# Two weight splits of a head pair placed behind the normalised q/k of its first and second tile, and the gate product made once for both heads on VectorE

## The chip, the cores and the metric

One core of a Trainium2 chip runs the whole program. The metric is device time in microseconds (us). All matrix products are made on TensorE (PE; PEld is its weight load), elementwise work on VectorE (DVE), ScalarE (ACT) and GpSimd (POOL); SyncE (SP) issues the loads from HBM. Each engine works through its own queue in order and waits there for the semaphores of the others.

## The reference

Two decoder layers over 512 tokens of width 1024. Each layer projects the normalised input to q, k, v and a gate for 16 heads of 64, runs two kinds of attention, multiplies by the gate, projects back and adds a gated embedding:

```
u = rms_norm(h, norm_g)
qa, ka, va, ga, fa, qb, kb, vb, gb = split(u @ w_in)
qa = rms_norm(heads(qa, 8), qk_g[0]);  ka = rms_norm(heads(ka, 8), qk_g[1])
oa = forgetting_attention(qa, ka, heads(va, 8), log_sigmoid(fa + b_f)) * silu(ga)
qb = partial_rope(rms_norm(heads(qb, 8), qk_g[2]));  kb likewise with qk_g[3]
ob = dilated_attention(qb, kb, heads(vb, 8)) * silu(gb)
h = h + concat([oa, ob]) @ w_out
h = h + (p_i @ w_ple) * sigmoid(rms_norm(h, ple_norm_g) @ w_ple_gate)
```

## The kernel before

**Precision.** Every float32 product is made of three matmuls. An operand is split into a high part (ScalarE, a rounding copy) and a low part (VectorE, the difference); `mm3` adds high x high, high x low and low x high. Activations live split in `X` and `Y` (high, low). Weights arrive in `raw` (3 buffers) and are split into `whi` (ScalarE, L157) and `wlo` (VectorE, L158), 5 buffers each. `W.pump()` makes the next split in a fixed list if its buffer is free; a split then also issues the load of a later `raw`.

**Head pairs.** A layer handles its 16 heads as 8 pairs `p`; pairs 0 to 3 are dilated (with rotary), 4 to 7 forgetting. The loop over `p` from 1 to 7 is a software pipeline: pair `p` is projected while the attention of pair `a = p - 1` is computed and that of pair `b = p - 2` is finished. A pair's weights are three pieces of w_q,k,v (1152, 1152 and 768 columns of `raw`) and one of the gate (1024). In the pass `p` the two "late" splits are those of the gate piece of `p` (1024) and of the first piece of pair `p + 1` (1152).

**The order on TensorE within a pass** is the order of the program (a wrapper keeps it): `pj(p, t)` projects the 128-token tile `t` onto 384 columns (24 matmuls). First `pj(p, 0)`, with `att_pv(b, 0)`, the product of probabilities and values of head 0 of pair `b`, inside it; then `pj(p, 1)` with `att_pv(b, 1)` inside; `pj(p, 2)`; `att_s(a)`, the scores of both heads of `a`; `pj(p, 3)`; `gate_mm`; and the transposes of the probabilities and of q and k (L91).

**The projections' results share two PSUM buffers**, `psA`. So `pj(p, 2)` may begin only when the first tile's result has been read, `pj(p, 3)` when the second's has, and the next pass's `pj(p + 1, 0)` when the gate's has (L482). A result is read by `ev(p, t)`: ScalarE squares it (L440, `sq`), VectorE reduces to mean squares (L442, L443, `ms`), GpSimd raises them to the power -1/2 (L445, `f`), and VectorE multiplies (L458, `z`). Beside this the value columns are scaled and split into `V2` (high L451 on ScalarE, low L452 on VectorE; two buffers by the parity of the pair, so that pair `p` overwrites what `att_pv(b, ...)` reads). Pairs below 4 then rotate `z` (L463 to L466; on GpSimd for tiles 0 to 2).

**Finishing pair b**: `att_pv` leaves a [128, 512] PSUM tile per head, whose two halves are added (L652 `ob` on ScalarE, L653 on VectorE) into 64 rows of `U[7]`; these rows are multiplied by the gate `U[5]` or `U[6]` (L655, a [64, 512] product per head, on GpSimd except for the last pair). `att_o` then splits `U[7]` into high (L658) and low (L659).

**Who sets the order on the other engines.** A scheduler orders each engine's instructions by program order and readiness. `with behind("A", "V")` ties instructions of the block behind the last instruction noted for ScalarE (`last["A"]`: L451 or a split of probabilities) and VectorE (`last["V"]`: L458, L482 or such a split). The closing step of the gate (L484, the function that `gate_evac` returns as `rest`) has no such tie.

Of the kernel before, what the change touches and what calls it, by code (L numbers as in the profile page):

```python
# [13 lines left out]
ALU = mybir.AluOpType  # L14
# [9 lines left out]
NPAIR = 8  # L24
# [177 lines left out]
def trunk(tc, ap):  # L202
    nc = tc.nc
    V, A, G, T = nc.vector, nc.scalar, nc.gpsimd, InOrder(tc, nc.tensor)
    ctx = ExitStack()
    with ctx:
# [11 lines left out]
        def ptile(pool, tag):  # L218
            return pool.tile([P, S], F32, tag=tag, name=tag)
# [19 lines left out]
        W = Weights(nc, wp, rp, specs)  # L239
# [4 lines left out]
        U = [cp.tile([P, S], F32, name=f"U{i}") for i in range(NK)]  # L244
# [128 lines left out]
        def behind(*engines):  # L373

            st = ExitStack()
            for e in engines:
                st.enter_context(tc.issue_after(last[e].ins))
            return st


        def square_acc(h, d, E=V):
            if d == 0:
                A.activation(acc, h, AF.Square)
            else:
                sq = tp.tile([P, S], F32, tag="sqh", name="sqh")
                done = A.activation(sq, h, AF.Square)
                E.tensor_tensor(acc, acc, sq, op=ALU.add)
                return done
# [7 lines left out]
        def finish_stats(pool, tag):  # L396
# [5 lines left out]
            r = sp.tile([P, NT], F32, tag="r", name="r")  # L402
            E = sp.tile([P, NT], F32, tag="E", name="E")
            rh = sp.tile([P, NT], F32, tag="rh", name="rh")
            V.tensor_scalar(m, ps[:, :NT], 1.0 / D, EPS, op0=ALU.mult, op1=ALU.add)  # L405
            G.tensor_tensor(r, m, mhalf.to_broadcast([P, NT]), op=ALU.pow)  # L406
            V.tensor_scalar(E, m, EPS, None, op0=ALU.mult)
            V.tensor_scalar(rh, r, 0.5, None, op0=ALU.mult)
            return r, E, rh

# [13 lines left out]
        def proj(l, p, t, u, ps, k0, k1):  # L424
            w = QW0 if p == 0 else QW
            for k in range(k0, k1):
                s, kk = min(k // 3, 2), k - 3 * min(k // 3, 2)
                wh, wl = W.get(("q", l, p, s))
                tk = slice(t * P, (t + 1) * P)
                mm3(ps[:, :w], u[0][:, k, tk], u[1][:, k, tk], wh[:, kk, :], wl[:, kk, :],  # L430
                    k == 0, k == NK - 1)
                if t == NT - 1 and k in (2, 5, 7):
                    W.done(("q", l, p, s))

        def evac_proj_a(l, p, t, ps, st):
# [6 lines left out]
            V.tensor_reduce(ms, sq, axis=AX.X, op=ALU.add)  # L442
            V.tensor_scalar(ms, ms, 1.0 / HD, st["E"][:, t:t + 1], op0=ALU.mult, op1=ALU.add)  # L443
            f = sp.tile([P, 4], F32, tag="f", name="f")
# [87 lines left out]
        def att_z(z):  # L532

            ps = pair(psM, "psM")
            for t in range(NT):
                for c in (0, 2):
                    o = (c // 2 * NT + t) * 64
                    flip([x[:, o:o + 64] for x in ps],
                         z[t][:, c:c + 2].rearrange("p h d -> p (h d)"))
            return ps  # L540
# [95 lines left out]
        def att_pv(a, j, pt=PT):  # L636
            ps = ptile(psS, "psS")
            v2 = V2[a % 2]
            for i in range(2):
                for kt in range(NT):  # L640
                    q0 = min(kt, 2)
                    if kt < 2:
                        rhs = pt[i][:, KOFF[kt]:KOFF[kt] + NT - kt]
                    elif kt == 2:
                        rhs = pt[i][:, 8:10 + 2 * j:1 + 2 * j]
                    else:
                        rhs = pt[i][:, 0:11 + 2 * j:10 + 2 * j]
                    T.matmul(ps[:, q0 * P:], v2[:, kt, j], rhs, start=(kt == 0 and i == 0),
                             stop=(kt == NT - 1 and i == 1))
            b = slice(64 * j, 64 * j + 64)  # L650
            tm = tp.tile([HD, S], F32, tag="ob", name="ob")
            A.activation(tm, ps[64:128], AF.Copy)  # L652
            V.tensor_tensor(U[7][b], ps[0:64], tm, op=ALU.add)  # L653
            E = V if a == NPAIR - 1 else G
            E.tensor_tensor(U[7][b], U[7][b], U[5 + a % 2][b], op=ALU.mult)  # L655

        def att_o(a, dst):
            A.activation(dst[0][:, a], U[7], AF.Copy)  # L658
            V.tensor_tensor(dst[1][:, a], U[7], dst[0][:, a].bitcast(F32), op=ALU.subtract)  # L659

# [24 lines left out]
        for l in range(DEPTH):  # L685
# [5 lines left out]
            def pj(p, t, k0=0, k1=NK):  # L691
                if k0 == 0:
                    cur[t] = ptile(psA, "psA")
                proj(l, p, t, u, cur[t], k0, k1)

            def ev(p, t):
                f = evac_proj_a(l, p, t, cur[t], st)
                zs[(p, t)] = evac_proj_b(l, p, t, cur[t], f)
# [45 lines left out]
            for p in range(1, NPAIR):  # L744
                a, b = p - 1, p - 2
                if p == 2:
                    log_forget(l)
                if p == 7 and l + 1 < DEPTH:
                    rope_tables(l + 1)
                if p == 1:  # L750
                    pj(p, 0)
                    pj(p, 1)
                    ev(p, 0)
                    att_qk(l, 0, att_z(zt(0)))
                    W.pump(2)
                else:
                    pj(p, 0, 0, 6)
                    att_pv(b, 0)
                    att_pt(1, tps)
                    with behind("A", "V"):  # L760
                        W.pump(2)
                    pj(p, 0, 6, NK)
                    pj(p, 1, 0, 3)
                    att_pv(b, 1)
                    pj(p, 1, 3, NK)
                    ev(p, 0)
                    att_o(b, oo)
                ev(p, 1)
                pj(p, 2)
                ev(p, 2)  # L770
                att_s(a)
                if NDIL <= p < NPAIR and a >= NDIL:
                    bias_rows(p)
                pj(p, 3)
                ev(p, 3)
                if p == NDIL:
                    cumulate()
                    bias_rows(p)
                gps = ptile(psA, "psA")
                gate_mm(l, p, u, gps, 0, NK)  # L780
                with behind("A", "V"):
                    W.pump()
                tps = [pair(psS, "psS") for _ in range(2)]
                att_tp(tps)
                pqk = att_z(zt(p))
                tpb = ptile(psA, "psA")
                att_tp2(tpb)
                rest = gate_evac(p, gps)
                att_pt(0, tps)
                att_pt2(tpb)  # L790
                with behind("A", "V"):
                    W.pump()
                att_qk(l, p, pqk)
                rest()

            a, b = NPAIR - 1, NPAIR - 2
            part(0, 0, 5)
# [166 lines left out]
```

## Time and profile before

| | |
|---|---|
| median of 3 runs | 768.87 us (761.44, 768.87 and 1137.11) |
| profiled execution | 761.52 us |
| its span, first to last instruction | 759.5 us |
| mean granted TensorE clock | 0.978 of full speed |
| PE busy | 711.9 us (94%) |
| DVE / ACT / POOL busy | 510.1 / 383.6 / 212.4 us |

The 2 us between the profiled execution's time and its span lie outside all instructions. The granted clock is a share of 2.4 GHz. Busy time is summed over stages that are bound by different things, so what a wait costs is read where it occurs.

### The profile page before, as it was taken

What the parts mean: (1) busy time and instruction counts of PE and PEld (TensorE: products, weight loads), DVE (VectorE), ACT (ScalarE), POOL (GpSimd) and SP (SyncE); (2) the same over time, 40 slices, a digit from 0 to 9 for tenths busy, and PEclk for the clock granted to TensorE, in tenths of its full rate; (3) what the DMA queues carried; (4) which work ended last, traced back from release to release, by engine and by line L of the source; (5) the groups of instructions that cost most, each with busy time, mean ns of one, the idle gap of its engine ahead of it and who ended that gap; (6) DMA issues with size and microseconds to landing.
All of it is one profiled execution on the core that took longest, in us unless ns stands there. A gap on an engine that the chain in (4) does not pass through costs nothing.

```text
span 759.5 us, 12111 instructions
## 1 busy us (share of the span) xinstructions
PE 711.9 (94%) x4424; PEld 630.7 (83%) x4424; DVE 510.1 (67%) x1228; ACT 383.6 (51%) x809; POOL 212.4 (28%) x354
## 2 busy tenths in 40 slices
PE   9998989897989899999999989898898989999997
PEld 8987979787978787887899889787787888888886
DVE  7878668675757486938737778585748577777443
ACT  8565546363736456625525647354545456564311
POOL 7363433322332511000004443524142323300000
PEclk9999999999999999999999999999999999999999
DMA  8513121212212043616323122120303031355211
GB/s 289 162 29 112 32 80 33 80 45 69 64 50 86 27 125 102 203 43 196 113 82 111 32 80 63 50 85 28 103 10 111 9 104 30 125 155 164 84 41 42
DMA packets 23946, 65.52 MB, mean 86 GB/s; under 512 B 4816, under 2 KB 6096, under 8 KB 23888
## 3 DMA queue, kind: packets, MB, share of 16 engines
q1 hardware_dynamic: 22576, 64.68, 27.4%
q8 instruction: 35, 0.57, 0.3%
q10 hardware_dynamic: 1312, 0.08, 0.1%
q14 instruction: 23, 0.19, 0.1%
HBM read 60.49 MB, written 4.19 MB: 85 GB/s over the span
## 4 chain that ended last, share of the span: by engine, by line
PE 71%; DVE 10%; ACT 8%; issue 5%; POOL 5%; ACTq 1%; DMA 0%; SPq 0%; POOLq 0%; DVEq 0%
PE psA L88 49%; PE psS L88 15%; PE psM L88 4%; DVE wlo L158 4%; POOL f L445 3%; ACT PT L621 2%; POOL U L655 2%; ACT whi L157 2%; ACT U L599 2%; PE psS L91 2%; DVE U L653 1%; PE psM L91 1%; DVE z L458 1%; ACT ob L652 1%; PE psA L91 1%
## 5 line engine op out<-in xcount | busy, mean ns | idle before, releaser
L88 PE MATMUL psA<-whi,X 128*128 128x384 f32 (+1 forms) x480 | 137.6, 355 | 20.5 <-DVE z L458 20.5
L88 PE MATMUL psA<-whi,Y 128*128 128x384 f32 (+1 forms) x480 | 135.1, 351 | 19.5 <-DVE z L458 19.5
L158 DVE TENSOR_TENSOR wlo<-raw,whi 128x1024 fp32r<-128x1024 f32 (+3 forms) x105 | 135.0, 1296 | 12.7 <-ACT whi L157 12.0
L157 ACT ACTIVATE whi<-raw 128x1024 fp32r<-128x1024 f32 (+3 forms) x105 | 105.4, 1020 | 68.5 <-PE psA L88 51.6
L88 PEld LDWEIGHTS psA<-whi,X 128*128 128x128 f32 x480 | 92.8, 199 | 23.7 <-issue 22.2
L88 PEld LDWEIGHTS psA<-whi,Y 128*128 128x128 f32 x480 | 91.3, 196 | 22.3 <-issue 21.3
L88 PE MATMUL psA<-Y,whi 128*128 128x512 f32 (+1 forms) x320 | 96.6, 385 | 0.5 <-DVE sqh L860 0.5
L88 PE MATMUL psA<-X,whi 128*128 128x512 f32 x304 | 95.7, 396 | 0.0
L655 POOL TENSOR_TENSOR U<-U,U 64x512 f32<-64x512 f32 x28 | 38.9, 1388 | 197.9 <-DVE U L653 197.9
L445 POOL TENSOR_TENSOR f<-ms,mhalf 128x4 f32<-128x4 f32 x64 | 64.7, 1011 | 97.1 <-DVE ms L443 87.3
L599 ACT ACTIVATE U<-U,mx 128x512 f32<-128x512 f32 (+3 forms) x128 | 70.6, 554 | 31.9 <-DVE mx L597 31.9
L88 PE MATMUL psA<-wlo,X 128*128 128x384 f32 (+1 forms) x240 | 84.5, 352 | 0.5 <-DVE wlo L158 0.5
L88 PE MATMUL psA<-wlo,Y 128*128 128x384 f32 (+1 forms) x240 | 83.3, 347 | 0.1
L601 POOL TENSOR_SCALAR U<-U,sm 128x512 f32<-128x512 f32 (+3 forms) x128 | 65.7, 533 | 25.5 <-DVE sm L600 25.2
L458 DVE TENSOR_TENSOR z<-psA,f 128x256 f32<-128x256 f32 x60 | 25.4, 424 | 66.3 <-POOL f L445 66.3
L88 PEld LDWEIGHTS psA<-Y,whi 128*128 128x128 f32 x320 | 58.4, 188 | 13.2 <-DVE sqh L860 1.2
L88 PEld LDWEIGHTS psA<-X,whi 128*128 128x128 f32 x304 | 56.5, 188 | 13.1 <-DVE sqh L860 0.5
L440 ACT ACTIVATE sq<-psA 128x256 f32<-128x256 f32 x56 | 21.3, 381 | 82.6 <-PE psA L88 76.3
L88 PE MATMUL psA<-Y,wlo 128*128 128x512 f32 (+1 forms) x160 | 61.3, 383 | 0.0
L88 PE MATMUL psA<-X,wlo 128*128 128x512 f32 x152 | 59.9, 394 | 0.0
L442 DVE TENSOR_REDUCE ms<-sq 128x4 f32<-128x256 f32 x56 | 23.3, 416 | 47.4 <-ACT sq L440 46.4
L406 POOL TENSOR_TENSOR r<-m,mhalf 128x4 f32<-128x4 f32 x4 | 4.7, 1184 | 161.1 <-DVE m L405 161.1
(191 smaller groups left out, 1319.9 us busy)
## 6 DMA issues: line engine op xcount, KB each, us to landing
raw<-in_wq_dram SPq DMA_DIRECT2D x28, 576.0 KB, 3.8
raw<-in_wg_dram SPq DMA_DIRECT2D x16, 512.0 KB, 4.2
raw<-in_wo_dram SPq DMA_DIRECT2D x16, 512.0 KB, 3.5
raw<-in_wpg_dram SPq DMA_DIRECT2D x16, 512.0 KB, 3.4
raw<-in_wq_dram SPq DMA_DIRECT2D x14, 384.0 KB, 3.1
U<-in_xT_dram SPq DMA_DIRECT2D x16, 256.0 KB, 3.7
raw<-in_wple_dram SPq DMA_DIRECT2D x4, 512.0 KB, 3.8
hs<-U SPq DMA_DIRECT2D x8, 256.0 KB, 3.1
```

The costliest lines, as they stand in the source:

```text
L88: return self.tc.keep_in_program_order(self.eng.matmul(*a, **k))
L91: return self.tc.keep_in_program_order(self.eng.transpose(*a, **k))
L157: self.nc.scalar.activation(hi, r, AF.Copy)
L158: eng.tensor_tensor(lo, r, hi.bitcast(F32), op=ALU.subtract)
L440: A.activation(sq, ps[:, :2 * P].rearrange("p (h d) -> p h d", h=4), AF.Square)
L442: V.tensor_reduce(ms, sq, axis=AX.X, op=ALU.add)
L445: G.tensor_tensor(f, ms, mhalf.to_broadcast([P, 4]), op=ALU.pow)
L458: last["V"] = V.tensor_tensor(z, ps[:, :2 * P].rearrange("p (h d) -> p h d", h=4), f[:, :, None].to_broadcast([P, 4, HD]), op=ALU.mult)
L599: A.activation(seg, seg, AF.Exp, bias=mx, scale=-1.0, accum_out=sm)
L601: G.tensor_scalar(seg, seg, sm, 1.0, op0=ALU.mult, op1=ALU.mult)
L621: last["A"] = A.activation(hi, src, AF.Copy)
L655: E.tensor_tensor(U[7][b], U[7][b], U[5 + a % 2][b], op=ALU.mult)
```

## The change

- `att_pv` no longer multiplies by the gate. `att_o` does it once, for both heads, as one [128, 512] product on VectorE in front of its two halves of the split.
- The two splits that `W.pump(2)` made ahead of the rest of `pj(p, 0)` are set apart: one behind the first tile's `ev`, one behind the second's, each tied behind that tile's L451 on ScalarE and L458 on VectorE.
- The closing step of the gate is tied behind the last instruction noted for VectorE.

```
             U[7][b] = ps[0:64] + tm
-            E = V if a == NPAIR - 1 else G
-            E.tensor_tensor(U[7][b], U[7][b], U[5 + a % 2][b], op=ALU.mult)
         def att_o(a, dst):
+            V.tensor_tensor(U[7], U[7], U[5 + a % 2], op=ALU.mult)
...
                     pj(p, 0, 0, 6)
                     att_pv(b, 0)
                     att_pt(1, tps)
-                    with behind("A", "V"):
-                        W.pump(2)
                     pj(p, 0, 6, NK)
...
                     ev(p, 0)
+                    with behind("A", "V"):
+                        W.pump()
                     att_o(b, oo)
                 ev(p, 1)
+                if p > 1:
+                    with behind("A", "V"):
+                        W.pump()
                 pj(p, 2)
...
                 att_qk(l, p, pqk)
-                rest()
+                with behind("V"):
+                    rest()
```

The order on TensorE, and that of the loads on SyncE, is the same in both kernels. On the other engines it moves. The names are the program's with a number: `U_95` is `U[7]`, `U_93` and `U_94` are the gates `U[5]` and `U[6]`, `Y_86` and `Y_87` the high and low part of `Y`, `V_116` a `V2` buffer.

VectorE in the pass p = 3 of the first layer, from the first head's sum to the low part of the attention output; first the kernel before:

```order
L653 TENSOR_TENSOR U_95<-psS,ob 64x512
L158 TENSOR_TENSOR wlo<-raw,whi 128x1024
L158 TENSOR_TENSOR wlo<-raw,whi 128x1152
L442 TENSOR_REDUCE ms<-sq 128x4
L653 TENSOR_TENSOR U_95<-psS,ob 64x512
L443 TENSOR_SCALAR ms<-ms,E 128x4
L452 SCALAR_TENSOR_TENSOR V_116<-psA,r,V_116 128x2x64
L458 TENSOR_TENSOR z<-psA,f 128x256
L659 TENSOR_TENSOR Y_87<-U_95,Y_86 128x512
```

The first tile's chain (L442, L443, L458) stands behind both splits and, by L443, behind the second head's sum. In the changed kernel:

```order
L653 TENSOR_TENSOR U_95<-psS,ob 64x512
L442 TENSOR_REDUCE ms<-sq 128x4
L443 TENSOR_SCALAR ms<-ms,E 128x4
L452 SCALAR_TENSOR_TENSOR V_116<-psA,r,V_116 128x2x64
L458 TENSOR_TENSOR z<-psA,f 128x256
L158 TENSOR_TENSOR wlo<-raw,whi 128x1024
L653 TENSOR_TENSOR U_95<-psS,ob 64x512
L656 TENSOR_TENSOR U_95<-U_95,U_94 128x512
L442 TENSOR_REDUCE ms<-sq 128x4
L452 SCALAR_TENSOR_TENSOR V_116<-psA,r,V_116 128x2x64
L443 TENSOR_SCALAR ms<-ms,E 128x4
L458 TENSOR_TENSOR z<-psA,f 128x256
```

The first tile's chain now precedes the 1024 split, and the product L656 stands ahead of the second tile's chain; the 1152 split and the low part (L658) follow behind that second L458.

ScalarE at the same place, before:

```order
L652 ACTIVATE ob<-psS 64x512
L157 ACTIVATE whi<-raw 128x1024
L157 ACTIVATE whi<-raw 128x1152
L440 ACTIVATE sq<-psA 128x256
L451 ACTIVATE V_116<-psA,r 128x2x64
L652 ACTIVATE ob<-psS 64x512
```

and in the changed kernel:

```order
L652 ACTIVATE ob<-psS 64x512
L440 ACTIVATE sq<-psA 128x256
L451 ACTIVATE V_116<-psA,r 128x2x64
L157 ACTIVATE whi<-raw 128x1024
L652 ACTIVATE ob<-psS 64x512
L440 ACTIVATE sq<-psA 128x256
L451 ACTIVATE V_116<-psA,r 128x2x64
L157 ACTIVATE whi<-raw 128x1152
```

Square and value copy of the first tile have come ahead of both high parts.

VectorE at the seam between two passes, from the gate's result (L482) to the split of the last weight piece (768), before:

```order
L482 TENSOR_TENSOR U_93<-psA,Rh 128x512
L484 SCALAR_TENSOR_TENSOR U_93<-sqh,U_93 128x512
L622 TENSOR_TENSOR PT_123<-psS,PT_122 128x8x64 x2
L549 SCALAR_TENSOR_TENSOR QQ_118<-psM,gq,QQ_117 128x4x64 x2
L622 TENSOR_TENSOR PT_123<-psA,PT_122 128x512
L158 TENSOR_TENSOR wlo<-raw,whi 128x768
```

and in the changed kernel:

```order
L482 TENSOR_TENSOR U_93<-psA,Rh 128x512
L622 TENSOR_TENSOR PT_123<-psS,PT_122 128x8x64 x2
L549 SCALAR_TENSOR_TENSOR QQ_118<-psM,gq,QQ_117 128x4x64 x2
L622 TENSOR_TENSOR PT_123<-psA,PT_122 128x512
L484 SCALAR_TENSOR_TENSOR U_93<-sqh,U_93 128x512
L158 TENSOR_TENSOR wlo<-raw,whi 128x768
```

The gate's closing step has gone from ahead of the split of the probabilities (L622) to behind it.

## Rows read from the trace of the kernel before

**Rows 1.** The page's list of engines: busy us, share of the span, instructions.

```profile
PE 711.9 (94%) x4424; PEld 630.7 (83%) x4424; DVE 510.1 (67%) x1228; ACT 383.6 (51%) x809; POOL 212.4 (28%) x354
```

**Rows 2.** Who waited for whom: us in total, times, the longest one.

```profile
PE psA L88 <- DVE z L458: 40.0, 12, 4.5
```

**Rows 3.** TensorE in the twelve stretches from the end of such a wait to the first score matmul (the 24 matmuls of pj(p, 2)): stretch, its us, PE busy (instructions), granted clock, DMA share, GB/s. The first and the last of nine at a clock below 1, the three at 1.00, and the sum of all twelve; then, from the same view, the 24 matmuls of pj(3, 3) in the first layer, ahead of which nothing waits.

```profile
73.29:79.21 5.92, 5.92 (x24) 0.71 0.00 1
...
249.68:254.05 4.37, 4.37 (x25) 1.00 0.00 0
447.90:452.27 4.37, 4.37 (x24) 1.00 0.02 4
...
587.04:592.72 5.68, 5.68 (x25) 0.75 0.01 3
621.76:626.13 4.37, 4.37 (x24) 1.00 0.01 2
sum 65.49, PE 65.47; mean PE 5.46
...
115.82:120.13 4.31, 4.31 (x27) 1.00 0.00 0
```

**Rows 4.** Timeline of TensorE in the pass p = 3 of the first layer: start us, us, engine, line, operation, out<-in, shape, count, [idle before <-releaser]. 93.34 begins pj(3, 0); 98.75 is its last matmul and the next one's first; 104.25 is the last of pj(3, 1); 107.76 the first of pj(3, 2); 113.68 begins the scores; 115.82 pj(3, 3).

```profile
93.34 0.43 PE L88 MATMUL psA<-whi,X 128*128 128x384 f32 x1
...
98.75 0.52 PE L88 MATMUL psA<-whi,X 128*128 128x384 f32 x2
...
100.50 1.46 PE L88 MATMUL psS<-PT,V 128*128 128x512 f32 x8
...
104.25 0.34 PE L88 MATMUL psA<-whi,X 128*128 128x384 f32 x1
107.76 0.41 PE L88 MATMUL psA<-whi,X 128*128 128x384 f32 x1 [3.17 <-DVE z L458]
...
113.68 1.50 PE L88 MATMUL psS<-KK,QQ 64*128 64x512 f32 x12
...
115.82 0.44 PE L88 MATMUL psA<-whi,X 128*128 128x384 f32 x1
```

**Rows 5.** Timeline of ScalarE in the same pass.

```profile
98.42 0.59 ACT L652 ACTIVATE ob<-psS 64x512 f32<-64x512 f32 x1
98.92 2.11 ACT L157 ACTIVATE whi<-raw 128x1024 fp32r<-128x1024 f32 x2
101.05 0.38 ACT L440 ACTIVATE sq<-psA 128x256 f32<-128x256 f32 x1
101.59 0.37 ACT L451 ACTIVATE V<-psA,r 128x128 fp32r<-128x128 f32 x1 [0.16 <-PE psS L88]
```

**Rows 6.** Timeline of VectorE in the same pass; the first two rows are of its beginning, the last of the third tile.

```profile
89.96 1.35 DVE L158 TENSOR_TENSOR wlo<-raw,whi 128x1152 fp32r<-128x1152 f32 x1
91.39 0.69 DVE L482 TENSOR_TENSOR U<-psA,Rh 128x512 f32<-128x512 f32 x1
92.78 0.69 DVE L484 SCALAR_TENSOR_TENSOR U<-sqh,U 128x512 f32<-128x512 f32 x1 [0.70 <-ACT sqh L483]
...
99.22 0.67 DVE L653 TENSOR_TENSOR U<-psS,ob 64x512 f32<-64x512 f32 x1
100.01 3.61 DVE L158 TENSOR_TENSOR wlo<-raw,whi 128x1024 fp32r<-128x1024 f32 x2
103.54 0.40 DVE L442 TENSOR_REDUCE ms<-sq 128x4 f32<-128x256 f32 x1
103.98 0.69 DVE L653 TENSOR_TENSOR U<-psS,ob 64x512 f32<-64x512 f32 x1
104.70 0.23 DVE L443 TENSOR_SCALAR ms<-ms,E 128x4 f32<-128x4 f32 x1
104.83 0.34 DVE L452 SCALAR_TENSOR_TENSOR V<-psA,r,V 128x128 fp32r<-128x128 f32 x1
107.19 0.42 DVE L458 TENSOR_TENSOR z<-psA,f 128x256 f32<-128x256 f32 x1 [2.01 <-POOL f L445]
107.53 0.68 DVE L659 TENSOR_TENSOR Y<-U,Y 128x512 fp32r<-128x512 f32 x1
...
114.20 0.42 DVE L442 TENSOR_REDUCE ms<-sq 128x4 f32<-128x256 f32 x1 [3.45 <-ACT sq L440]
```

**Rows 7.** Timeline of GpSimd in the same pass.

```profile
99.98 1.29 POOL L655 TENSOR_TENSOR U<-U,U 64x512 f32<-64x512 f32 x1 [11.24 <-DVE U L653]
104.81 1.26 POOL L655 TENSOR_TENSOR U<-U,U 64x512 f32<-64x512 f32 x1 [3.54 <-DVE U L653]
106.15 1.01 POOL L445 TENSOR_TENSOR f<-ms,mhalf 128x4 f32<-128x4 f32 x1
```

**Rows 8.** Groups of instructions by line and shape (busy us, mean ns | idle before): a VectorE step of the new product's shape, both inputs in SBUF.

```profile
L387 DVE TENSOR_TENSOR acc<-acc,sqh 128x512 f32<-128x512 f32 x28 | 19.3, 689 | 0.0
```

**Rows 9.** Timeline at the seam from the pass p = 3 to p = 4: the gate's result on VectorE and the first matmul of pj(4, 0) on TensorE.

```profile
126.55 0.69 DVE L482 TENSOR_TENSOR U<-psA,Rh 128x512 f32<-128x512 f32 x1
...
127.88 0.42 PE L88 MATMUL psA<-whi,X 128*128 128x384 f32 x1
```

**Rows 10.** Timeline inside pj(5, 0): the low part of the weight piece of 768 columns on VectorE and the first matmul that reads it.

```profile
167.73 0.96 DVE L158 TENSOR_TENSOR wlo<-raw,whi 128x768 fp32r<-128x768 f32 x1
...
168.75 0.44 PE L88 MATMUL psA<-wlo,X 128*128 128x384 f32 x1 [0.32 <-DVE wlo L158]
```

More of the change, by code (lines that the diff above doesn't have):

```diff
@@ L653, in att_pv @@
             V.tensor_tensor(U[7][b], ps[0:64], tm, op=ALU.add)
-            E = V if a == NPAIR - 1 else G
-            E.tensor_tensor(U[7][b], U[7][b], U[5 + a % 2][b], op=ALU.mult)
         def att_o(a, dst):
+            V.tensor_tensor(U[7], U[7], U[5 + a % 2], op=ALU.mult)
             A.activation(dst[0][:, a], U[7], AF.Copy)
@@ L759, in trunk @@
                     att_pt(1, tps)
-                    with behind("A", "V"):
-                        W.pump(2)
                     pj(p, 0, 6, NK)
@@ L766, in trunk @@
                     ev(p, 0)
+                    with behind("A", "V"):
+                        W.pump()
                     att_o(b, oo)
                 ev(p, 1)
+                if p > 1:
+                    with behind("A", "V"):
+                        W.pump()
                 pj(p, 2)
@@ L793, in trunk @@
                 att_qk(l, p, pqk)
-                rest()
+                with behind("V"):
+                    rest()
             a, b = NPAIR - 1, NPAIR - 2
```

## The prediction, made before the changed kernel ran

> **What bounds the kernel now.** I read the list of engines first. TensorE is busy for 711.9 of 759.5 us, VectorE for 510.1 [rows 1], so the time is TensorE's work plus its idle time, and a change on the other engines counts only through the latter. The list of waits says where that idle time is: twelve waits for the product z, 40.0 us together, the longest 4.5 [rows 2]. Twelve is six passes (p = 2 to 7) in two layers, one wait in each. Then I read the stretch behind each wait, because TensorE's clock need not be the same there: in nine of the twelve the 24 matmuls of pj(p, 2) ran with a granted clock of 0.71 to 0.75, that is partly at the lower level, 1.2 GHz, and partly at 2.4, and took 5.92 us in the first and 5.68 in the last of them; in the other three the clock was 1.00 and they took 4.37 [rows 3]. All twelve took 65.49; at 4.37 each they would take 52.44. So 13.05 us of slow matmuls go with the 40.0 of waiting.
>
> Last I read one pass, p = 3 of the first layer, on all four engines, to see what makes z late. TensorE ends pj(3, 1) at 104.59 and could begin pj(3, 2) at 104.42, one matmul spacing after the start of its last; it begins at 107.76, after z [rows 4]. The result that z reads was complete at about 99.1, where pj(3, 0) ended [rows 4]. Its chain starts late on ScalarE: the square waits behind both weights' high parts (2.11 us) and starts at 101.05 [rows 5]. It starts later still on VectorE, where both low parts run from 100.01 for 3.61 us and the reduction begins at 103.54; then the second head's sum (0.69) stands between L442 and L443. And on GpSimd the power waits for the second head's gate product, from 104.81 for 1.26, and starts at 106.15 [rows 6, 7]. Each of the three steps of the change takes one of these obstacles away.
>
> **The first tile's chain in the new order**, p = 3, with the durations of these rows.
> - ScalarE: ob ends at 99.01 [rows 5], the square runs 99.1 to 99.5. The value copy L451 doesn't move forward: it overwrites the buffer that att_pv of pair 1 is reading, and in the trace it was released by that product at 101.59 [rows 5]. So L451 ends at 101.96 in both orders.
> - VectorE: the first head's sum ends at 99.89, L442 takes 0.40 and L443 0.23 [rows 6], which with the hops of some 0.1 gives 100.7. GpSimd's power takes 1.01 [rows 7]: 101.8. L452 (0.34), ahead of z in the queue, has to wait for L451 and ends at 102.3; z takes 0.42 [rows 6] and ends at about 102.8.
> - TensorE wants the buffer at 104.42. The margin is 1.6 us; the wait goes altogether.
>
> **What lands behind it.** ScalarE makes the 1024 high part after L451 (half of 2.11, so until 103.0) and ob of the second head until 103.6. VectorE makes the low part: two took 3.61 us beside a GpSimd product, one of 1152 alone 1.35 [rows 6], so a single one lies between 1.35 and 1.9. I take 1.35, since GpSimd's product is gone: 104.4. The second sum (0.69) gives 105.1. The new product isn't in the trace; the nearest row of its shape, both inputs in SBUF, takes 0.689 [rows 8], and from below a half-height sum that reads PSUM 0.67 [rows 6], so 0.69: 105.8. Then L442, L452, L443 and the power: 108.0, and z of the second tile at 108.4. TensorE needs it for pj(3, 3). Without the wait pj(3, 2) runs from 104.42 for 4.31 to 4.37 [rows 3], the scores take 2.14 (113.68 to 115.82 [rows 4]), so at 110.9. The margin is 2.5.
>
> **The product.** GpSimd's two of 1.26 and 1.29 go [rows 7], VectorE gets one of 0.69. It costs nothing while it lies inside that margin of 2.5; uncovered, it would cost 12 x 0.69 = 8.3. For the last pair of each layer two half products on VectorE become one, with nothing to hide them: one less of about 0.69 for each layer on VectorE, but the first could already run ahead of the second sum, so I count nothing there.
>
> The trace shows the two engines in each other's way: two low parts took 3.61 with a product beside them, and at the pace of one alone would take 2.7 [rows 6, 7]. The Trainium skill, page Perfetto Trace Analysis, section Optimizing Scalar/DVE Operations, warns that GpSimd and VectorE share an SBUF read port, so that moving work between them might not help; on the contention these rows agree with it. By that rule the 1.26 that the power waited for would stay in the chain, 12 x 1.26 = 15.1 us less gain, and the sum would come to about 724. I don't take it, because the order puts the product behind the first tile's z.
>
> **The second split and the seam.** Behind the second z (108.4) VectorE has the 1152 low part (1.35) and the attention's low part (0.68): 110.4. The third tile's square is ready at about 109.3, so its L442 is up to 1.1 late; in the trace VectorE had been idle for 3.45 us ahead of this instruction [rows 6], and that idle time is the cover. The rows also overlap by up to 0.1 each, which would leave 0.3. A delay here passes on through softmax and the fourth tile to L482, which must free the buffer for the next pass. There the margin is 1.26 (L482 ends at 92.08, TensorE begins at 93.34 [rows 4, 6]), and 0.64 at the seam to p = 4, where it ends at 127.24 and TensorE begins at 127.88 [rows 9]. So a stall of between 0 and 0.5 us there; I take 0, and 12 x 0.5 = 6 as the upper end.
>
> **The gate's closing step** (0.69) leaves the head of the seam, along with the idle 0.70 in front of it [rows 6], so the splits of the probabilities may start 1.4 us earlier and absorb a late L482. It now stands ahead of the 768 low part, on which TensorE waited 0.32 in one pass [rows 10]; I allow 0.3 more in each layer, 0.6 together. Nobody needs its result until the product two passes on.
>
> **Loads.** The split of 1024 is followed by the load of the 768 piece of the next pair, which is split only after the next L482 (126.55 [rows 9]), some 20 us later; the one of 1152 by the load of the next gate, which is split a pass later. That both go out 2 to 9 us later costs nothing; a load that came too late would show as ScalarE waiting for it.
>
> **The sum**, against the profiled execution: 761.52 - 40.0 (waits) - 13.05 (slow matmuls) + 0.6 = 709.1. I say **709 us**. That execution equals the fastest of the three runs (761.44); the median (768.87) is 1% higher, and a median of the changed kernel may lie as much above my sum, at 716. The other ends: everything as bounded above without the seam and with VectorE's overlaps in my favour, 705; all seams at 0.5, 715.
>
> **Rivals.**
> - *The wait shrinks but stays.* z of the first tile hangs on L452, which hangs on ScalarE's L451, which hangs on TensorE's att_pv; if any of these falls behind by more than the 1.6 us of margin, TensorE still waits. For it speaks that L451 was released by TensorE in the trace [rows 5]; against it, that nothing but the square stands ahead of it now. At 1 us of waiting in each of twelve passes the sum is 721. I count no slow matmuls behind so short a wait: even of the twelve waits of the trace, 3.3 us in the mean, three were followed by a clock of 1.00 [rows 3].
> - *The clock stays low.* The nine slow stretches have another cause than the wait ahead of them, and only the 40.0 come back: 721.5. Against it: each of the nine follows a wait, and pj(3, 3), which nothing holds up, takes 4.31 us at a clock of 1.00 [rows 3].
> - *The splits move the wait to the seam: slower than before.* The two low parts and the product are 1.35 + 1.35 + 0.69 = 3.4 us of VectorE's time, 4.3 if the splits take 3.61 as beside GpSimd. If none of it fits into idle time, the third tile's chain, softmax and L482 are late by 4.3, TensorE waits 3.0 to 3.7 at each seam, the clock falls again (1.3 to 1.55 per pass), and that is 12 x 4.9 = 59 paid for 53 gained: 767. It decides from a delay of about 3.9 at the third tile's L442, where 3.45 us of idle time speak against it [rows 6].
>
> **Chances.** Forecast 0.78, the wait that stays 0.12, the clock 0.06, slower 0.04. The range from 704 to 723 takes in the first three down to the upper bounds and leaves out the last and a part of the second, some 0.12. A measurement of this kernel tells about 2% from no change. All cases but the last are 5% or more faster; the last lies within 2% or just beyond. So faster 0.95, same 0.04, slower 0.01.
>
> **What would show it.** In the trace of the changed kernel the waits of TensorE for z should be gone from the list, or far below 40; the mean granted clock should rise from 0.978 to nearly 1; a pass should take about 29.7 instead of 34.5 us (93.34 to 127.88 [rows 4, 9], less 3.17 and 1.55); L440 of the first tile should follow pj(p, 0) by under 0.1 us, and z should end 1 to 2 us before pj(p, 1) does. Of the seam: the time from L482's end to the next pass's first matmul, 1.26 before, should stay above zero, and the idle time ahead of the third tile's L442 should nearly vanish. The prediction is wrong if new waits for L482 or for a weight's low part appear in every pass, if the granted clock stays low in places without a wait, or if z of the first tile turns out to wait for something that these rows don't show, a PSUM or V2 buffer above all.

## The result, and the profile of the changed kernel

The changed kernel takes 712.23 us (711.52 to 713.09 in four runs), against 767.11 for the kernel before, the median of four runs, of which one took 1137.11. The ratio, which leaves that run out, is 0.931, with a 95% interval from 0.925 to 0.937: 6.9% less time. The prediction was 709, with a range from 704 to 723. The profiled execution took 712.22 us, its span is 710.4, and the granted clock is 0.999 in the mean, as foreseen.

The list of engines, as [rows 1]:

```profile
PE 699.4 (98%) x4424; PEld 618.4 (87%) x4424; DVE 501.8 (71%) x1240; ACT 382.3 (54%) x809; POOL 182.9 (26%) x326
```

TensorE does the same 4424 matmuls in 12.5 us less, and its idle time has gone from 47.6 us (759.5 less 711.9) to 11.0. Who waited for whom, TensorE's list from its top (us in total, times, longest), as [rows 2]:

```profile
PE psA L88 <- DVE wlo L158: 2.9, 8, 0.6
PE psM L88 <- DVE QQ L303: 1.5, 1, 1.5
PE psS L88 <- DVE PT L622: 0.6, 3, 0.2
```

The twelve waits for z, 40.0 us, are gone from the list. What heads it now is small: eight waits for a weight's low part, one ahead of the first pass and seven in the twelve passes. The matmuls that followed the waits, as [rows 3] (stretch of pj(p, 2), us, PE busy, clock, DMA share, GB/s; that of p = 3 in the first layer, the last, and the sum of the twelve):

```profile
99.81:104.11 4.30, 4.30 (x26) 1.00 0.34 91
...
572.24:576.55 4.31, 4.31 (x26) 1.00 0.39 122
sum 51.52, PE 51.52; mean PE 4.29
```

All twelve run at a clock of 1.00, at 2.4 GHz, and take 51.52 us instead of 65.49. They are even 0.9 below the 52.44 that the prediction took, for without a wait ahead of it each takes about 4.3, as pj(3, 3) did before [rows 3], and not 4.37.

The first tile's chain in the pass p = 3 of the first layer. ScalarE, as [rows 5], with the third tile's square as its last row:

```profile
94.52 0.38 ACT L440 ACTIVATE sq<-psA 128x256 f32<-128x256 f32 x1
96.97 0.37 ACT L451 ACTIVATE V<-psA,r 128x128 fp32r<-128x128 f32 x1 [2.07 <-PE psS L88]
97.24 1.05 ACT L157 ACTIVATE whi<-raw 128x1024 fp32r<-128x1024 f32 x1
...
104.22 0.39 ACT L440 ACTIVATE sq<-psA 128x256 f32<-128x256 f32 x1 [1.99 <-PE psA L88]
```

VectorE, as [rows 6], from the first tile's L443 to the third tile's reduction, and then the seam to p = 4 and the place in p = 6 that an experiment below is compared with:

```profile
96.22 0.23 DVE L443 TENSOR_SCALAR ms<-ms,E 128x4 f32<-128x4 f32 x1
97.37 0.35 DVE L452 SCALAR_TENSOR_TENSOR V<-psA,r,V 128x128 fp32r<-128x128 f32 x1 [0.92 <-ACT V L451]
97.64 0.41 DVE L458 TENSOR_TENSOR z<-psA,f 128x256 f32<-128x256 f32 x1
98.32 1.23 DVE L158 TENSOR_TENSOR wlo<-raw,whi 128x1024 fp32r<-128x1024 f32 x1 [0.26 <-ACT whi L157]
...
100.30 0.70 DVE L656 TENSOR_TENSOR U<-U,U 128x512 f32<-128x512 f32 x1
...
102.86 0.42 DVE L458 TENSOR_TENSOR z<-psA,f 128x256 f32<-128x256 f32 x1 [1.13 <-POOL f L445]
103.20 1.35 DVE L158 TENSOR_TENSOR wlo<-raw,whi 128x1152 fp32r<-128x1152 f32 x1
...
105.12 0.41 DVE L442 TENSOR_REDUCE ms<-sq 128x4 f32<-128x256 f32 x1
...
117.58 0.68 DVE L482 TENSOR_TENSOR U<-psA,Rh 128x512 f32<-128x512 f32 x1
...
183.73 0.68 DVE L622 TENSOR_TENSOR PT<-psA,PT 128x512 fp32r<-128x512 f32 x1
184.33 0.68 DVE L484 SCALAR_TENSOR_TENSOR U<-sqh,U 128x512 f32<-128x512 f32 x1
184.93 0.95 DVE L158 TENSOR_TENSOR wlo<-raw,whi 128x768 fp32r<-128x768 f32 x1
```

TensorE, as [rows 4] and [rows 9]: the first matmul of pj(3, 0), the first of pj(3, 3), the first of pj(4, 0), and in p = 6 the first that reads the 768 low part:

```profile
88.69 0.43 PE L88 MATMUL psA<-whi,X 128*128 128x384 f32 x1
...
106.24 0.44 PE L88 MATMUL psA<-whi,X 128*128 128x384 f32 x1
...
118.41 0.41 PE L88 MATMUL psA<-whi,X 128*128 128x384 f32 x1
...
185.94 0.44 PE L88 MATMUL psA<-wlo,X 128*128 128x384 f32 x1 [0.39 <-DVE wlo L158]
```

The first z ends at 98.05 and pj(3, 2) begins at 99.81, 1.76 later. L451 waited 2.07 us for TensorE's att_pv, with the square done long before, as foreseen. The second z ends at 103.28, and pj(3, 3) wants its buffer at 106.24. From pj(3, 0) to pj(4, 0) the pass takes 29.72 us, where it took 34.54. At the seam L482 ends at 118.26 and TensorE goes on at 118.41, 0.15 later; before, the margin there was 0.64 [rows 9]. Nothing is to spare at 0.15: as much lies between z and the matmul that waited for it in the kernel before (107.61 to 107.76 [rows 4, 6]).

Since TensorE's order is the same in both kernels, the spacing of each two matmuls in a row can be compared from start to start, which accounts for the 49.1 us by which the span fell: -41.9 for z, -12.4 for the matmuls that ran at the lower clock, +3.2 for the weights' low parts (all but 0.1 of it for the 768 piece), +1.1 and +0.4 for the splits of the probabilities (L622, L621), +0.8 for L482. The 0.3 that is left lies in spacings too small to name.

### The profile page after: what moved, and what is told of

The parts are those of the page before. It is cut to its first block, busy times and chain, and to the rows that moved or that the text cites. A ratio compares the mean times of both kernels' runs of the same rounds, so it can differ in the third digit from the quotient of the medians.

```text
span 710.4 us, 12211 instructions
## 1 busy us (share of the span) xinstructions
PE 699.4 (98%) x4424; PEld 618.4 (87%) x4424; DVE 501.8 (71%) x1240; ACT 382.3 (54%) x809; POOL 182.9 (26%) x326
## 4 chain that ended last, share of the span: by engine, by line
PE 64%; DVE 17%; ACT 8%; issue 4%; POOL 4%; ACTq 2%; DMA 0%; POOLq 0%; DVEq 0%
PE psA L88 42%; PE psS L88 16%; DVE wlo L158 5%; PE psM L88 4%; POOL f L445 3%; DVE PT L622 3%; ACT U L599 3%; ACTq L523 2%; ACT PT L621 1%; DVE U L597 1%; DVE U L653 1%; ACT whi L157 1%; ACT sqh L483 1%; DVE V L452 1%; DVE ms L442 1%
## 5 line engine op out<-in xcount | busy, mean ns | idle before, releaser
L158 DVE TENSOR_TENSOR wlo<-raw,whi 128x1024 fp32r<-128x1024 f32 (+3 forms) x105 | 122.8, 1171 | 13.3 <-ACT whi L157 13.2
L88 PE MATMUL psA<-whi,X 128*128 128x384 f32 (+1 forms) x480 | 130.5, 341 | 0.0
L88 PE MATMUL psA<-whi,Y 128*128 128x384 f32 (+1 forms) x480 | 129.3, 341 | 0.2 <-DVE U L482 0.2
L88 PEld LDWEIGHTS psA<-whi,X 128*128 128x128 f32 x480 | 87.9, 188 | 1.8 <-ACT whi L157 0.5
L88 PEld LDWEIGHTS psA<-whi,Y 128*128 128x128 f32 x480 | 87.5, 188 | 1.4 <-issue 0.4
L88 PE MATMUL psA<-wlo,X 128*128 128x384 f32 (+1 forms) x240 | 81.8, 341 | 1.7 <-DVE wlo L158 1.7
L88 PE MATMUL psA<-wlo,Y 128*128 128x384 f32 (+1 forms) x240 | 81.3, 339 | 1.2 <-DVE wlo L158 1.2
L458 DVE TENSOR_TENSOR z<-psA,f 128x256 f32<-128x256 f32 x60 | 25.4, 423 | 45.9 <-POOL f L445 45.9
L622 DVE TENSOR_TENSOR PT<-psS,PT 128x512 fp32r<-128x512 f32 (+1 forms) x58 | 37.1, 673 | 19.1 <-ACT PT L621 19.1
L88 PEld LDWEIGHTS psA<-wlo,X 128*128 128x128 f32 x240 | 45.2, 188 | 3.2 <-DVE wlo L158 3.2
L88 PEld LDWEIGHTS psA<-wlo,Y 128*128 128x128 f32 x240 | 45.1, 188 | 2.0 <-DVE wlo L158 2.0
```

The source lines that it names most:

```text
L88: return self.tc.keep_in_program_order(self.eng.matmul(*a, **k))
L158: eng.tensor_tensor(lo, r, hi.bitcast(F32), op=ALU.subtract)
L458: last["V"] = V.tensor_tensor(z, ps[:, :2 * P].rearrange("p (h d) -> p h d", h=4), f[:, :, None].to_broadcast([P, 4, HD]), op=ALU.mult)
L622: last["V"] = V.tensor_tensor(lo, src, hi.bitcast(F32), op=ALU.subtract)
```

## The experiments

Three questions. Which of the three parts of the change brings the gain? Which part gives some of it back in the new waits, and can it be had again? And are the margins what the prediction said? Times are medians; the kernel before took 766.2 to 767.4 beside them.

### The splits apart, without the other two parts

```
 (the changed kernel, with the product and the closing step as before)
             V.tensor_tensor(U[7][b], ps[0:64], tm, op=ALU.add)
+            E = V if a == NPAIR - 1 else G
+            E.tensor_tensor(U[7][b], U[7][b], U[5 + a % 2][b], op=ALU.mult)
         def att_o(a, dst):
-            V.tensor_tensor(U[7], U[7], U[5 + a % 2], op=ALU.mult)
...
-                with behind("V"):
-                    rest()
+                rest()
```

> The two splits are set apart as in the change, but the gate product stays per head on GpSimd and the gate's closing step is not tied. Theory (the splits alone held z of the first tile up; the product only added to it): z of the first tile ends before pj(p, 1) does, though GpSimd's first product may put the power off by 0.7 us; the twelve waits and the slow matmuls go, 712 us give or take 2. Rival (the product on GpSimd holds z up by itself, 1.26 us in each pass): TensorE still waits about 1 us in each of twelve passes, 722 to 727 us.

711.59 us (710.88 to 711.94), ratio 0.930 (0.924 to 0.935). So the splits alone bring all that the whole change brings; nothing of the waits for z remains. The margin of the first z is smaller, though, down to 0.27 and 0.30 us in the passes p = 5, and a reason is seen in this kernel's trace, p = 3. VectorE:

```profile
95.61 1.02 DVE L443 TENSOR_SCALAR ms<-ms,E 128x4 f32<-128x4 f32 x1
...
100.65 1.18 DVE L443 TENSOR_SCALAR ms<-ms,E 128x4 f32<-128x4 f32 x1
```

and GpSimd:

```profile
95.33 1.28 POOL L655 TENSOR_TENSOR U<-U,U 64x512 f32<-64x512 f32 x1 [10.67 <-DVE U L653]
...
100.51 1.29 POOL L655 TENSOR_TENSOR U<-U,U 64x512 f32<-64x512 f32 x1
```

L443, a step on four columns that takes 0.23 us in the changed kernel, starts just after GpSimd's product and ends when the product ends (96.63 and 96.61; 101.83 and 101.80). It stands still for the rest of it.

### The product alone

```
 (the kernel before)
             V.tensor_tensor(U[7][b], ps[0:64], tm, op=ALU.add)
-            E = V if a == NPAIR - 1 else G
-            E.tensor_tensor(U[7][b], U[7][b], U[5 + a % 2][b], op=ALU.mult)
         def att_o(a, dst):
+            V.tensor_tensor(U[7], U[7], U[5 + a % 2], op=ALU.mult)
```

> Only the product moves to VectorE, both splits stay ahead of the first tile's chain. Theory: the power of the first tile starts when L443 ends, 1.2 us earlier, so the twelve waits shrink from 40 to about 25 us in all but stay; and since the slow matmuls belong to the length of the wait ahead of them, waits of 2 us leave the clock at 1.00 and 13 us come back too: about 734 us. Rival (the clock falls whatever the wait's length): 747 us. Second rival (moving work between GpSimd and VectorE brings nothing): 761 us.

729.40 us (728.05 to 730.52), ratio 0.953 (0.946 to 0.960), 5 us better than the expectation had it, with 16.8 us of waiting where it had 25. TensorE's list of waits, its first line:

```profile
PE psA L88 <- DVE z L458: 16.8, 12, 2.8
```

VectorE in p = 3, both splits (the row has two instructions) and L443:

```profile
97.96 2.50 DVE L158 TENSOR_TENSOR wlo<-raw,whi 128x1024 fp32r<-128x1024 f32 x2
...
101.53 0.23 DVE L443 TENSOR_SCALAR ms<-ms,E 128x4 f32<-128x4 f32 x1
```

and GpSimd's power for the first tile of that pass:

```profile
101.84 1.01 POOL L445 TENSOR_TENSOR f<-ms,mhalf 128x4 f32<-128x4 f32 x1 [15.12 <-DVE ms L443]
```

The two splits take 2.50 instead of 3.61 [rows 6], and the power starts after L443 and no longer behind a product of 1.26 [rows 7]. So the two products on GpSimd held z up twice in this pass: 1.1 us on VectorE, where the first split stood still beside the first product, and about 1.2 in GpSimd's own queue. Ten of the twelve passes look like it; in those of p = 2 both delays are shorter. As an estimate, 12 x 2.3 = 28 us is therefore an upper end, against 23.2 less waiting (40.0 to 16.8). Matched matmul by matmul with the kernel before, 11.1 of the 32.9 us between the two spans are the clock. Two of the twelve stretches of pj(p, 2); the second is the only slow one:

```profile
72.78:77.14 4.36, 4.36 (x25) 1.00 0.01 6
168.82:174.74 5.92, 5.92 (x24) 0.71 0.05 20
```

Alone the splits gain 55 us and the product 37, both together 58 (the run without the tie, below): they remove the same wait. Once the splits are apart, the product's place is worth little.

### The tie of the closing step alone

```
 (the kernel before)
                 att_qk(l, p, pqk)
-                rest()
+                with behind("V"):
+                    rest()
```

> The kernel before with only the gate's closing step tied behind the split of the probabilities. Theory: the twelve waits for z are untouched, and what little TensorE waits for the 768 low part is absorbed by them: 761 us give or take 2. Rival (the 1.4 us that the head of the seam gains carry through to z): 745 us.

759.27 us (756.92 to 765.50), ratio 0.992 (0.989 to 0.996): 0.8% less time, well below 2% but beyond its interval. The time is the expected one, the reason is not quite: the waits for z, which were to be untouched, fall from 40.0 to 32.8 us. All the same, ten of the twelve stretches behind them now run partly at the lower clock, where it was nine. Two of them, with their granted clock:

```profile
178.36:182.72 4.36, 4.36 (x25) 1.00 0.01 4
210.99:216.88 5.89, 5.89 (x25) 0.72 0.00 1
```

and the waits ahead of these two, from TensorE's timeline:

```profile
178.36 0.41 PE L88 MATMUL psA<-whi,X 128*128 128x384 f32 x1 [3.05 <-DVE z L458]
...
210.99 0.66 PE L88 MATMUL psA<-whi,X 128*128 128x384 f32 x1 [2.26 <-DVE z L458]
```

The longer wait is followed by the full clock, the shorter one by the lower. So the length of a wait doesn't decide by itself whether the clock falls behind it.

### The change without the tie

```
 (the changed kernel)
                 att_qk(l, p, pqk)
-                with behind("V"):
-                    rest()
+                rest()
```

> The change without the tie of the gate's closing step. Theory A (the step in front of the 768 low part is what makes TensorE wait 2.9 us for that part): the waits for the 768 low part fall back to about 0.6 us and the time is 709 to 711 us. Theory B (L482 comes late at the seam now, 0.1 to 0.9 us ahead of TensorE instead of 0.6 to 1.3, and the closing step at the head of the seam would wait 0.7 for ScalarE and put off the splits of the probabilities and the 768 low part by up to 1.4): the waits grow, 715 us or more.

708.48 us (708.00 to 709.75), ratio 0.926 (0.921 to 0.930). Beside the changed kernel on one chip it is 708.92 against 712.75 (below). The tie, which takes 0.8% off the kernel before, costs the changed one 3.8 us. TensorE's list of waits, the line on the low parts:

```profile
PE psA L88 <- DVE wlo L158: 0.8, 3, 0.3
```

VectorE in p = 6, to be held against the same place in the changed kernel (183.73 to 184.93 above):

```profile
181.21 0.69 DVE L484 SCALAR_TENSOR_TENSOR U<-sqh,U 128x512 f32<-128x512 f32 x1 [0.70 <-ACT sqh L483]
...
183.80 0.68 DVE L622 TENSOR_TENSOR PT<-psA,PT 128x512 fp32r<-128x512 f32 x1
184.40 0.95 DVE L158 TENSOR_TENSOR wlo<-raw,whi 128x768 fp32r<-128x768 f32 x1
```

and TensorE:

```profile
185.41 0.44 PE L88 MATMUL psA<-wlo,X 128*128 128x384 f32 x1
```

Without the tie L484 is over before the probabilities' split; with it, it stands straight ahead of the 768 low part, which TensorE needs next, and moves it back by 0.5 us relative to the pass's begin. In five of the eight waits of the changed kernel (p = 4, 6 and 7 in the first layer, 6 and 7 in the second) L484 is the instruction ahead of the split. In the two of p = 5, 0.58 us each, it is a second L549, which has moved ahead of the split; the eighth, 0.20, lies before the first pass and is there in the kernel before too.

This run and the one with the splits alone differ only in the product, and neither has the tie: 708.48 against 711.59, on one chip. That is the product's worth once the splits are apart: 3.1 us.

### One split ahead of the first tile, or both behind the second

The 1024 split back in its old place:

```
                     att_pt(1, tps)
+                    with behind("A", "V"):
+                        W.pump()
                     pj(p, 0, 6, NK)
...
                     ev(p, 0)
-                    with behind("A", "V"):
-                        W.pump()
                     att_o(b, oo)
```

> The change, but the split of 1024 goes back to its old place ahead of the first tile's chain; only the one of 1152 stays behind z of the second tile. Theory (z of the first tile has 1.1 to 1.8 us of margin in the profile of the changed kernel, and ScalarE's value copy, which waits for TensorE, hides most of a split): z comes up to 1.4 us later, so TensorE waits 0 to 0.3 us per pass, and the time is 711 to 715 us. Rival (each split ahead of the chain costs its own length): 12 x 1.3 us more, about 728 us.

717.68 us (717.49 to 718.26), ratio 0.939 (0.933 to 0.946): 2.7 us above the expectation. The list shows no wait for z; its margin is 0.15 to 0.83 us, thinner by up to about the length of the split, and in the three passes where it is 0.15 the matched matmuls behind it lose 0.2 us each. Most of the loss is elsewhere, by TensorE's list of waits:

```profile
PE psA L88 <- DVE wlo L158: 3.3, 8, 0.6
PE psA L88 <- DVE U L482: 1.7, 3, 0.7
```

Both behind the second tile:

```
                     ev(p, 0)
-                    with behind("A", "V"):
-                        W.pump()
                     att_o(b, oo)
...
                     with behind("A", "V"):
-                        W.pump()
+                        W.pump(2)
```

> The change, but both splits stand behind z of the second tile. Theory (the seam is the next tight place: L482 ends only 0.1 to 0.9 us ahead of TensorE's next matmul in the changed kernel): the third tile's chain, softmax and L482 come about 1.3 us later, TensorE waits some 0.4 to 1.2 us at each of twelve seams, 720 to 725 us, with waits for L482 in the list. Rival (idle time of VectorE ahead of the third tile still covers it): 712 us as the change.

718.76 us (718.02 to 719.03), ratio 0.940 (0.935 to 0.946): 6.5 us lost against the changed kernel, 3.2 of it at the first matmul behind L482, as expected in kind and less in size (720 to 725). TensorE's list:

```profile
PE psA L88 <- DVE wlo L158: 3.9, 9, 0.6
PE psA L88 <- DVE U L482: 2.1, 3, 1.0
```

So there is a place for one split behind each tile and for no second one behind the second: two together there make the third tile's chain late (in p = 3 its L442 starts 17.5 us after the pass's begin instead of 16.4), and that is passed on to L482, as the prediction's seam step has it.

Why one split ahead of the first tile is nearly as dear, its trace shows in part. Matched with the changed kernel, 2.4 of its 5.4 us lie at the first matmul behind L482 and 0.6 at z; the rest is spread over smaller waits. VectorE and, at the seam behind it, TensorE in its pass p = 3:

```profile
101.37 0.69 DVE L658 TENSOR_TENSOR Y<-U,Y 128x512 fp32r<-128x512 f32 x1 [0.70 <-ACT Y L657]
...
119.04 0.41 PE L88 MATMUL psA<-whi,X 128*128 128x384 f32 x1 [0.44 <-DVE U L482]
```

The attention's low part (L658) has come to stand ahead of the second tile's chain, where VectorE idles 0.70 us for ScalarE's high part; in the changed kernel it stands behind the 1152 split and waits for nothing. From the pass's begin the second z ends 1.0 us later and L482 0.6 later than in the changed kernel. The same 0.70 stands in all twelve passes of both runs, so not all that either loses is the split's own length; no run here takes the two apart.

### The gate's tanh and closing step behind the 768 split

If VectorE's order ahead of the 768 split is what costs, ScalarE's should too: the tanh (L483) stands ahead of that split's high part and of the copies of the probabilities.

```
 (the changed kernel)
             last["V"] = V.tensor_tensor(gt, ps, Rh, op=ALU.mult)
-            A.activation(th, gt, AF.Tanh)
-            return lambda: V.scalar_tensor_tensor(gt, th, 1.0, gt, op0=ALU.add, op1=ALU.mult)
+
+            def close():
+                A.activation(th, gt, AF.Tanh)
+                V.scalar_tensor_tensor(gt, th, 1.0, gt, op0=ALU.add, op1=ALU.mult)
+            return close
...
-                with behind("V"):
+                with behind("A", "V"):
                     rest()
```

> The change, but the gate's tanh on ScalarE goes with its closing step behind the split of the 768 piece. Theory (the waits for the 768 low part come from what stands ahead of it at the head of the seam): the splits of the probabilities start 0.6 us earlier, the waits for the 768 low part go, and the time is 707 to 709 us, as without the tie or a little better. Rival (the tie itself isn't what costs): 712 us.

706.37 us (705.93 to 707.23), ratio 0.925 (0.921 to 0.929), 0.6 us below the 707 that was expected at best. Only one wait for a low part of a pass is left in its list:

```profile
PE psA L88 <- DVE wlo L158: 0.2, 1, 0.2
```

and in p = 6, VectorE's order is (L486 is the closing step here):

```profile
182.22 0.68 DVE L625 TENSOR_TENSOR PT<-psA,PT 128x512 fp32r<-128x512 f32 x1
182.82 0.94 DVE L158 TENSOR_TENSOR wlo<-raw,whi 128x768 fp32r<-128x768 f32 x1
...
184.47 0.68 DVE L486 SCALAR_TENSOR_TENSOR U<-sqh,U 128x512 f32<-128x512 f32 x1
```

The split comes 3.3 us after the pass's begin instead of 5.2 (its end less the first matmul of pj(6, 0), which is at 180.47 here and at 180.71 in the changed kernel).

### On top of that, the attention output's split later

The margin at L482 is still 0.15 to 0.9 us there (from the pass p = 2 on). Moving att_o from behind the first tile to the fourth (between its value copy and its z) takes its three steps out of the third tile's way.

```
 (the kernel with the late tanh)
                     ev(p, 0)
                     with behind("A", "V"):
                         W.pump()
-                    att_o(b, oo)
...
+                f3 = evac_proj_a(l, p, 3, cur[3], st)
+                if p > 1:
+                    with behind("W"):
+                        att_o(b, oo)
+                zs[(p, 3)] = evac_proj_b(l, p, 3, cur[3], f3)
```

> As the one with the late tanh, and the gate product with the split of the attention output moved on from behind the first tile to the fourth tile, where VectorE waits for GpSimd's power. Theory (what keeps L482 late is the work ahead of the third tile's chain): the third tile's chain and softmax start 0.5 us earlier, the seam's margins come back to 0.5 us or more, and the time falls by about 1 us more, to 706 to 708 us. Rival (the two steps then stand ahead of L482 and take the margin again): 709 us or more.

710.18 us (709.77 to 711.00), ratio 0.929 (0.925 to 0.934): 3.8 worse than without, and the rival was right. In the fourth tile these steps stand in VectorE's queue ahead of L482, whose margin falls to 0.05 to 0.59 us. Of the 2.8 us between the two profiles 1.4 lie at the first matmul behind L482 and most of the rest at splits of the probabilities. The idle time that the third tile gains is not the one that the seam needs.

### The same three on one chip

The changed kernel, the one without the tie and the one with the late tanh once more, side by side.

> The changed kernel itself once more, beside the next two on the same chip: 712 us.

> The change without the tie of the gate's closing step, once more: 708.5 us, 3 to 4 us below the change, if what was measured before isn't the difference between two chips; level with it otherwise.

> The change with the gate's tanh and closing step both behind the 768 split, once more: 706 to 707 us, 5 to 6 us below the change and 2 below the one without the tie; level with them if the differences are the chips'.

712.75 (711.88 to 713.77), 708.92 (708.09 to 710.10) and 706.38 (705.82 to 707.07); the ratios to the kernel before are 0.931 (0.927 to 0.934), 0.926 (0.922 to 0.929) and 0.922 (0.919 to 0.925). The times of the three don't overlap. The late tanh is the best version found, 0.9% below the changed kernel.

## Why the prediction was right, and where its terms were off

**What bounds the kernel.** Right. Idle time of TensorE and its clock behind the waits were the whole of it: -41.9 and -12.4 by the matched matmuls, against -40.0 and -13.05.

**The first tile's chain.** Right, step by step. The margin of z was put at 1.6 us; in p = 3 it is 1.76, and 1.1 to 1.8 over the twelve passes. The square follows pj(p, 0) at once, L451 waits for TensorE as it did before, and it is L452 behind it that z follows. The rival in which the wait stays hung on this margin, and needed it to vanish.

**What lands behind it.** The second z was to have 2.5 us to spare and has 3.0 (103.28 against 106.24). A single split takes 1.23 and 1.35 (I took 1.35 for both), and the product 0.70 (0.69).

**The product.** Its cost was put at nothing, and that is right. What I did not price is its old place: undone alone it is worth 37 us, and 3.1 once the splits are apart. The rival that I worked out there, in which 1.26 us a pass stay, did not come: with the product alone on VectorE the power starts at 101.84, 0.08 us behind L443. The sentence of the Trainium skill that I set beside it (page Perfetto Trace Analysis, section Optimizing Scalar/DVE Operations), that moving work between GpSimd and VectorE might not help, is not borne out here. What the rows show is that L443 ended with GpSimd's product, at 96.63 and 96.61. The Trainium skill, page SBUF — State Buffer, section Who interferes with whom, says this more exactly: where the two need the same ports, the one that issues second is blocked until the other has ended.

**The seam.** The direction was right and so was the mechanism: the third tile's L442 started 0.5 us after its square (105.12 against 104.61; foreseen 0.3 to 1.1), and L482's margin fell at nearly every seam, from 0.64 to 0.15 at that to p = 4. The stall that I took as 0 is 0.8 by matched matmuls, and the splits of the probabilities behind it add 1.5. Both stay within the 6 that I had as the upper end. The rival that moves the wait to the seam needed 3.9 us of delay at L442. The 29.7 us that I gave for a pass don't follow from the terms beside them (34.54 less 3.17 and 1.55 is 29.82); that 29.72 was measured is luck: by the matched matmuls each wait for z cost some 0.16 more than the list has (41.9 against 40.0).

**The closing step.** This is the term that was mis-sized: 0.6 for both layers, and the matched matmuls give 3.2, of which 2.3 lie in the five passes where L484 stands straight ahead of the split and 0.8 in those of p = 5. So one sign that I had named for being wrong came in part: new waits for a low part, in seven passes of twelve. I had the mechanism, that it comes to stand ahead of the 768 low part, but took one row as the measure, a wait of 0.32 in one pass [rows 10], as though the other passes had room. Ahead of the probabilities' split L484 fills time in which VectorE waits for their high part. Behind it, it lies on a path without room: in p = 6 and without the tie the 768 split ends at 185.35, 0.06 us ahead of the matmul that reads it, and L484 takes 0.68. Taking the tie out of the changed kernel gives 3.8 us back, which is a little more than the miss.

**The loads.** Right: that the weights are asked for later costs nothing. ScalarE's splits wait 6.0 us for loads in the whole kernel, against 6.9 before.

**The sum.** 709.1 against 712.22 for the profiled execution, 3.1 short: the waits for z and the slow matmuls gave 1.3 more than taken, the low parts took 2.6 more, L482 and the probabilities 2.3 that I had left out. That makes 3.6; the 0.5 by which it is too much lies in spacings too small to name and outside the span. Since the median of the changed kernel equals its profiled run, the 1% that I allowed for the median was not needed. The range held; the chances of the rivals can't be judged by one case.

## What to carry to other kernels

Work that lies in front of a result that frees a PSUM buffer can cost up to its length in each pass, and behind that result it may cost nothing: look for splits and products that stand between a matmul and the step that reads it, and set them behind that step one at a time, each into the idle time of one tile. When the big wait is gone, the next thing, here, is what stands ahead of the next weight's split; a step whose result is wanted late (here the gate's closing and its tanh) belongs behind it on both engines, and whether a step moved there has room is read in every pass and not in one. Parts of a change that remove the same wait are not to be added up: 55 and 37 made 58.

## What the runs showed of the hardware

VectorE and GpSimd can stop each other until the other's instruction ends, in both directions. L443 on VectorE took 1.02 and 1.18 us beside a product of GpSimd (the splits without the other two parts), and 0.23 without one. GpSimd's rotary step on 32 columns beside the 1024 split, in the changed kernel's p = 3:

```profile
98.13 0.25 POOL L463 TENSOR_TENSOR tm<-z,Sg 128x32 f32<-128x32 f32 x1 [0.60 <-DVE z L458]
98.34 1.31 POOL L464 TENSOR_TENSOR tm<-z,Sg 128x32 f32<-128x32 f32 x1
```

The split began at 98.32 and ended at 99.55; the step, the same in shape as the one ahead of it, began at 98.34 and ended at 99.65. A small instruction in a chain can thus become as slow as the long one that happens to run on the other engine.

The lower clock follows waits, and not by their length alone: after 2.26 us of waiting the 24 matmuls took 5.89 at a clock of 0.72 (partly at 1.2 GHz, partly at 2.4), after 3.05 they took 4.36 at 1.00, in one trace (the tie alone). What else decides it stays open; no run here was made for it. In the changed kernel, where no wait inside a pass is longer than 0.6 us, none of the twelve stretches was slow.
